# The MLP of a streaming encoder step as seven half-size block products instead of eight, tokens in halves, activations kept in DRAM

## The chip, the cores and the metric

The kernel runs on one core of one Trainium2 chip. The metric is the device time of one execution in microseconds (us). Its engines are TensorE (PE in the profile, its weight loads are PEld), VectorE (DVE), ScalarE (ACT), GpSimd (POOL) and SyncE (SP, which here only issues DMAs). Each engine takes its instructions in the order in which the program lists them.

## The reference

One layer of a hybrid encoder on 1024 prompt tokens and 32 sample tokens, in float32. What the change touches is the end of the layer:

```python
x = x + m                                    # m: output of the mixer
hm = rmsnorm(x, norm2_g[l]) @ w_mlp1[l]      # 1024 -> 4096
x = x + jnp.square(jax.nn.relu(hm)) @ w_mlp2[l]   # 4096 -> 1024
...
return rmsnorm(x, final_g), ...
```

## The kernel before

All activations are kept transposed: features on the 128 partitions, the 1056 tokens along the free axis. `R` holds the residual, 8 feature tiles by 1056 tokens. The tokens are taken in three chunks of 352 (`CW`).

The dense work is one stream of jobs. A job is a tile of 128 output features; its weights come as one DMA of 512 KB (`raw`), and are split into a high part `whi` (ACT, line 105) and the rest `wlo` (line 106, POOL at first, DVE in the second half of the program). The operand is split the same way, so that one float32 product becomes three passes (high by high, high by rest, rest by high). `group` (line 141) runs one job on one chunk: 8 tiles of the contraction by 3 passes, 24 matmuls of 352 columns into one of three PSUM banks; then the job's `evac` takes the sums out. `run` issues the loads and splits of the next two jobs ahead of a job's groups, and steps generators that stand beside the stream (`norm2`, `final`).

At the end of the program come 8 jobs for `w_o` (line 804: plus the input, into `R`; lines 213 and 214: split operands `h2`, by the gain of the norm; lines 789 to 793: sums of squares), then the MLP: four times 8 jobs of the first product (line 829: relu and the token's 1/rms; 831: square; 836 and 837: split into `u`) and 8 of the second (line 848: the sum is added into `R`). So the MLP is 64 jobs by 3 groups by 24 matmuls = 4608, and the last two jobs take their third chunk in halves of 176 columns. The hidden activations `u` stay on the chip, 1024 features at a time. Nothing of the residual goes through DRAM.

A token's 1/rms (`rstd_bc`) is a chain over four engines: small matmuls `st` (line 195), DVE `nv` (198), POOL `pow` into `nr` (200), DVE `dg` or `fbc` (204), matmuls `bc` (208).

The whole program stands in an order written out by hand; no scheduler moves anything.

Of the kernel before, what the change touches and what calls it, by code (L numbers as in the profile page):

```python
# [14 lines left out]
P = 128  # L15
# [5 lines left out]
NCH = 3  # L21
CW = T // NCH
HW = CW // 2
# [20 lines left out]
# Jobs beside the heads: conv pairs "c" and merge gates "g"; the first list stands before the heads, each other  # L44
# beside one head's retention.
# [13 lines left out]
def encoder_step(ctx: ExitStack, tc: tile.TileContext, xT, par_d, idn_d, cst_d, rot_d, w_in, w_co, w_ro,  # L59
                 w_o, w_1, w_2, sconv_d, sret_d, yT, oconv, oret):  # L60
    nc = tc.nc
    # Chunks of tokens; the last two are the halves of the third.
    cs = [slice(c * CW, (c + 1) * CW) for c in range(NCH)] + [slice(T - CW, T - HW), slice(T - HW, T)]
# [17 lines left out]
    ysp = [dram.tile([P, T], F32, name=f"ysp{i}") for i in range(8)]  # L81

# [25 lines left out]
    # Work beside the stream: generators that go on by a step after each group; those in `mids` also halfway.  # L108
# [9 lines left out]
    # Products whose evacuation waits for the first norm; ends of evacuations that come a group later.  # L118
    held, deferred, normed = [], [], [0]
    room = {}  # L120

# [4 lines left out]
    def group(n, c):  # L126
        j = jobs[n]
        xh, xl = j.rhs()
        if c < NCH:
            xh, xl, w = xh[c], xl[c], CW  # L130
        else:
            w = HW
            xh, xl = (a[NCH - 1][:, :, (c - NCH) * HW:(c - NCH + 1) * HW] for a in (xh, xl))
        ps = room.pop((n, c), None)
        if ps is None:
            ps = pm.tile([P, CW], F32, tag="pm", name=f"ps{n}_{c}")[:, :w]
# [15 lines left out]
    # Orders of two jobs' groups: chunk by chunk, and with the first job's end (and its weights' room) drawn forward.  # L152
# [3 lines left out]
    def run(count, order=None):  # L156
        """The next `count` jobs, job by job, or in the given order of (job, chunk)."""
# [53 lines left out]
    def gain_split(hi, lo, src, gcol):  # L211
        """src by the per-feature gain, split into hi and lo; the token's 1/rms comes after the product."""
# [26 lines left out]
    def finish(g):  # L239
        """What a generator returns at its end."""  # L240
# [6 lines left out]
    with tc.manual_schedule():  # L247
        xv = xT.rearrange("k p t -> p k t")
        with ExitStack() as ph:
# [43 lines left out]
            def gate_head(h):  # L293
                """The retention's own gate: swish, times the normed retention, in place."""
# [98 lines left out]
            def mm3(out, ws, xs, start, stop):  # L393
                """One product of split operands, as three passes."""
# [128 lines left out]
            def enter(c):  # L523
                """Chunk c's operands, and its squares."""
# [27 lines left out]
            def turn(c):  # L552
                """The rotary tables take the token's 1/rms."""
# [34 lines left out]
            # The jobs' order: conv pairs and merge gates around the heads' projections.  # L588
# [223 lines left out]
        def norm2():  # L812
            for _ in range(3):
                yield
# [201 lines left out]
```

## Time and profile before

| what | value |
| --- | --- |
| runs | 2277.15, 2277.15, 2273.67 us; median 2277.15 us |
| profiled execution | span 2274.5 us; no time of its own is listed beside the span |
| mean granted TensorE clock | 0.997 |
| steps of the `w_o` jobs | about 1430 to 1526 us |
| first split of `u` (line 836) | 1526.8 us |
| last matmul of the second product | 2262.6 us |

The profile's page gives busy time by engine, the span in 40 slices, the chain of work that ended last, and groups of instructions by line with the mean duration of one. A matmul's duration is longer than the distance to the next one, since they overlap; the rate is the number of them in a window. "Idle before" is how long an engine waited ahead of such an instruction, and for whom.

### The profile page before, as it was taken

What the parts mean: (1) busy time and instruction counts of PE and PEld (TensorE: products, weight loads), DVE (VectorE), ACT (ScalarE), POOL (GpSimd) and SP (SyncE); (2) the same over time, 40 slices, a digit from 0 to 9 for tenths busy, and PEclk for the clock granted to TensorE, in tenths of its full rate; (3) what the DMA queues carried; (4) which work ended last, traced back from release to release, by engine and by line L of the source; (5) the groups of instructions that cost most, each with busy time, mean ns of one, the idle gap of its engine ahead of it and who ended that gap; (6) DMA issues with size and microseconds to landing.
All of it is one profiled execution on the core that took longest, in us unless ns stands there. A gap on an engine that the chain in (4) does not pass through costs nothing.

```text
span 2274.5 us, 32748 instructions
## 1 busy us (share of the span) xinstructions
PE 2234.4 (98%) x13894; PEld 2190.3 (96%) x13894; DVE 1197.1 (53%) x1636; ACT 565.5 (25%) x969; POOL 759.0 (33%) x546
## 2 busy tenths in 40 slices
PE   7999999999999999999999999999999999999998
PEld 6999999999999999999999999999999999999998
DVE  7948885287943879359654663442222222222234
ACT  4113210132111321123243332333203202302321
POOL 4625465264642656436410542002102101201201
PEclk9999999999999999999999999999999999999999
DMA  4112122111211122211441333321111111111112
GB/s 165 50 45 67 39 103 75 38 57 59 100 59 48 48 68 84 66 48 56 162 167 57 128 111 95 95 66 47 47 47 47 47 47 47 47 47 47 47 47 77
DMA packets 60707, 159.12 MB, mean 70 GB/s; under 512 B 9744, under 2 KB 26384, under 8 KB 60560
## 3 DMA queue, kind: packets, MB, share of 16 engines
q1 hardware_dynamic: 60560, 157.02, 21.3%
q8 instruction: 109, 1.79, 0.3%
q14 instruction: 38, 0.31, 0.0%
HBM read 126.61 MB, written 30.39 MB: 69 GB/s over the span
## 4 chain that ended last, share of the span: by engine, by line
PE 87%; DVE 8%; issue 2%; POOL 1%; DMA 1%; ACT 0%; SPq 0%; DVEq 0%; ACTq 0%; POOLq 0%
PE ps L141 79%; DVE yc L364 4%; PE po L396 3%; PE pkv L396 2%; DVE o L305 1%; PE pto L490 1%; DVE h_lo L214 1%; POOL wlo L106 1%; PE pt L412 1%; PE pk L420 1%; DMA raw<-w_in 0%; DVE gsig L300 0%; DVE sq L539 0%; SPq L633 0%; PE pk L418 0%
## 5 line engine op out<-in xcount | busy, mean ns | idle before, releaser
L141 PE MATMUL ps<-h_hi,whi 128*128 128x352 f32 x1904 | 621.5, 326 | 7.9 <-ACT h_hi L213 6.7
L141 PE MATMUL ps<-h_hi,wlo 128*128 128x352 f32 x1904 | 615.9, 323 | 5.5 <-POOL wlo L106 4.8
L141 PE MATMUL ps<-h_lo,whi 128*128 128x352 f32 x1904 | 613.7, 322 | 0.7 <-DVE h_lo L214 0.7
L364 DVE SCALAR_TENSOR_TENSOR yc<-glu,par,yc 128x1086 f32<-128x1086 f32 x240 | 420.9, 1754 | 3.4
L141 PEld LDWEIGHTS ps<-h_hi,whi 128*128 128x128 f32 x1904 | 359.0, 189 | 12.1 <-ACT h_hi L213 6.7
L141 PE MATMUL ps<-u,whi 128*128 128x352 f32 (+1 forms) x1568 | 369.7, 320 | 0.0
L141 PEld LDWEIGHTS ps<-h_hi,wlo 128*128 128x128 f32 x1904 | 359.3, 189 | 7.8 <-POOL wlo L106 6.8
L141 PE MATMUL ps<-h,whi 128*128 128x352 f32 x1536 | 366.4, 322 | 0.0
L141 PEld LDWEIGHTS ps<-h_lo,whi 128*128 128x128 f32 x1904 | 360.7, 189 | 3.3 <-DVE h_lo L214 2.0
L105 ACT CAST whi<-raw 128x1024 fp32r<-128x1024 f32 x176 | 184.0, 1045 | 586.3 <-PE ps L141 469.1
L106 POOL TENSOR_TENSOR wlo<-raw,whi 128x1024 fp32r<-128x1024 f32 x80 | 232.4, 2906 | 193.7 <-ACT whi L105 193.7
L837 POOL TENSOR_TENSOR u<-uu,u 128x352 fp32r<-128x352 f32 x96 | 90.9, 947 | 551.8 <-ACT u L836 543.2
L141 PEld LDWEIGHTS ps<-u,whi 128*128 128x128 f32 x1568 | 269.4, 188 | 0.0
L141 PEld LDWEIGHTS ps<-h,whi 128*128 128x128 f32 x1536 | 265.2, 188 | 0.0
L141 PE MATMUL ps<-u,wlo 128*128 128x352 f32 (+1 forms) x784 | 249.4, 318 | 0.0
L141 PE MATMUL ps<-h,wlo 128*128 128x352 f32 x768 | 245.8, 320 | 0.0
L106 DVE TENSOR_TENSOR wlo<-raw,whi 128x1024 fp32r<-128x1024 f32 x96 | 117.9, 1228 | 127.7 <-ACT whi L105 118.8
L848 DVE TENSOR_TENSOR R<-ps,R 128x352 f32<-128x352 f32 (+1 forms) x98 | 50.6, 517 | 226.2 <-PE ps L141 226.2
L829 DVE SCALAR_TENSOR_TENSOR ur<-ps,rms 128x352 f32<-128x352 f32 x96 | 50.3, 524 | 214.1 <-PE ps L141 214.0
L141 PEld LDWEIGHTS ps<-u,wlo 128*128 128x128 f32 x784 | 147.0, 188 | 0.0
L141 PEld LDWEIGHTS ps<-h,wlo 128*128 128x128 f32 x768 | 143.9, 187 | 0.0
L831 ACT ACTIVATE uu<-ur 128x352 f32<-128x352 f32 x96 | 47.8, 498 | 245.8 <-DVE ur L829 245.8
(176 smaller groups left out, 3017.5 us busy)
## 6 DMA issues: line engine op xcount, KB each, us to landing
raw<-w_in SPq DMA_DIRECT2D x80, 512.0 KB, 4.1
raw<-w SPq DMA_DIRECT2D x64, 512.0 KB, 3.5
gate<-gt SPq DMA_DIRECT2D x16, 528.0 KB, 3.0
gsp<-o SPq DMA_DIRECT2D x16, 528.0 KB, 3.0
raw<-w_ro SPq DMA_DIRECT2D x16, 512.0 KB, 4.0
xt<-xT SPq DMA_DIRECT2D x12, 352.0 KB, 7.8
g0raw<-gsp SPq DMA_DIRECT2D x6, 704.0 KB, 9.8
gld<-gsp SPq DMA_DIRECT2D x12, 352.0 KB, 4.7
```

The source lines that it names most:

```text
L105: nc.scalar.copy(j.hi, j.raw)
L106: j.eng.tensor_tensor(out=j.lo, in0=j.raw, in1=j.hi.bitcast(F32), op=ALU.subtract)
L141: nc.tensor.matmul(ps, lhsT=a[:, k, :], rhs=x[:, k, :], start=(k == 0 and m == 0), stop=(k == KT - 1 and m == 2))
L214: nc.vector.scalar_tensor_tensor(out=lo, in0=src, scalar=pcol(gcol), in1=hi.bitcast(F32), op0=ALU.mult, op1=ALU.subtract)
L305: nc.vector.scalar_tensor_tensor(out=o[:, e, cs[c]], in0=y, scalar=pcol(O_GN + 4 * h + e), in1=t, op0=ALU.mult, op1=ALU.mult)
L364: nc.vector.scalar_tensor_tensor(out=y, in0=glu[:, t:t + YL], scalar=w, in1=y, op0=ALU.mult, op1=ALU.add)
L396: nc.tensor.matmul(out, lhsT=w, rhs=x, start=start and i == 0, stop=stop and i == 2)
L412: nc.tensor.transpose(pt[:n, e * P:(e + 1) * P], v[:, e, ts_], ident)
L829: nc.vector.scalar_tensor_tensor(out=r, in0=ps, scalar=0.0, in1=rms2[c], op0=ALU.max, op1=ALU.mult)
L831: nc.scalar.activation(out=u, in_=r, func=AF.Square)
L837: nc.gpsimd.tensor_tensor(out=lo[c][:, f, :], in0=u, in1=hi[c][:, f, :].bitcast(F32), op=ALU.subtract)
L848: nc.vector.tensor_tensor(out=R[:, f, cs[c]], in0=ps, in1=R[:, f, cs[c]], op=ALU.add)
```

## The change

The first product X1 = W1 X and the second Y = W2 U are each cut into blocks. A block product of the first one takes half of the contraction (4 tiles), half of the output features and half of the tokens (528); 2 by 2 by 2 halves would be eight block products, and Strassen's scheme in Winograd's form forms seven, from sums of blocks of the weights (S1 to S4) and of the operand (T1 to T4). A half of the tokens is run as two pieces of 264 columns (`s` = 0, 1), so one group is now 4 tiles by 3 passes = 12 matmuls of 264 columns.

- **`w_o`**: 16 jobs in place of 8, each on one half of the tokens (2 groups of 24 matmuls of 264 columns). `R` is also written to DRAM (`rsp`).
- **First product**: 16 pairs of feature tiles; a pair is 7 products by 2 pieces by 12 = 168 matmuls. The names are m*n*_*p**s*: pair n, product p, piece s. `operands` builds B22, T1 to T4 of the second token half from `R` (four differences of 128x4x264 on DVE, five splits on ACT with POOL or DVE) while products 1 and 2 of the first two pairs run; product 2 adds onto product 1 in the same PSUM bank, after ACT has copied product 1 out. From then on `R` is the place where the sums of a pair are collected (`U`, 8 tiles by 264): ACT takes relu and square, POOL forms the T sums, and one DMA writes them to DRAM (`usp`). The next pair uses the same place.
- **Second product**: 4 groups of features by 7 products = 28 slots, each 8 groups of 12 matmuls. The activations come back from DRAM (`xs`), are split on ACT, POOL and DVE; weight blocks are summed on DVE (`wsum`); the sums go into `R` and `acc` on DVE and POOL (`acc_r`, `acc_a`).
- The norm's gain is applied to `R` before the product, not after. The end (`ending`) is by quarters of 264 tokens.
- PSUM: five banks in turn in place of three.

```diff
-        h2 = [[], []]
...
+        def product(ps, w, x, fresh=True):
+
+            for k in range(QW):
+                for m, (a, b) in enumerate(((w[0], x[0]), (w[0], x[1]), (w[1], x[0]))):
+                    nc.tensor.matmul(ps, lhsT=a[:, k, :], rhs=b[:, k, :], start=(fresh and k == 0 and m == 0),
+                                     stop=(k == QW - 1 and m == 2), skip_group_check=not fresh)
+
+        def split2(w, src, eng):
+            nc.scalar.copy(w[0], src)
+            eng.tensor_tensor(out=w[1], in0=src, in1=w[0].bitcast(F32), op=ALU.subtract)
...
+        run_order = []
+        for n in range(2):
+            run_order += [(n, p, s) for p in (1, 2) for s in range(2)]
+        for n in range(2):
+            run_order += [(n, p, s) for s in range(2) for p in (3, 6, 5, 7, 4)]
+        for n in range(2, NPAIR):
+            run_order += [(n, p, s) for s in range(2) for p in (1, 6, 2, 5, 7, 3, 4)]
...
+                    def relu2():
+                        if n < 2:
+                            nc.scalar.activation(out=u[0], in_=e[:, 0], func=AF.Relu)
+                        nc.scalar.activation(out=U[:, 1:4], in_=U[:, 1:4], func=AF.Relu)
+                        nc.scalar.activation(out=U[:, 0:4], in_=U[:, 0:4], func=AF.Square)
+
+                    def ts():
+                        gt = nc.gpsimd.tensor_tensor
+                        gt(out=U[:, 4:6], in0=U[:, 1:3], in1=U[:, 0:2], op=ALU.subtract)
+                        gt(out=u[6], in0=u[2], in1=u[4], op=ALU.subtract)
+                        gt(out=u[7], in0=u[6], in1=u[3], op=ALU.subtract)
+                        nc.sync.dma_start(out=usp[n // 4][:, :, n % 4, s * ST:(s + 1) * ST], in_=U)
+                    hook(1, relu2)
+                    hook(2, ts)
...
+                scale_rows(range(4, 8), q, bc)
+                cut("B22", b22, nc.gpsimd)
+                if q == 2:
+                    next(rr[3])
+                scale_rows(range(4), q, bc)
+                tt(out=b11, in0=b12, in1=b11, op=ALU.subtract)
+                cut("T1", b11, nc.gpsimd)
+                tt(out=b12, in0=b22, in1=b12, op=ALU.subtract)
+                tt(out=b22, in0=b22, in1=b11, op=ALU.subtract)
+                tt(out=b21, in0=b22, in1=b21, op=ALU.subtract)
+                cut("T2", b22, nc.vector)
+                cut("T3", b12, nc.gpsimd)
+                cut("T4", b21, nc.vector)
...
+                if n >= 2 and s == 0:
+                    if p == 1:
+                        load_raw(m + 1)
+                        if n == 4:
+                            for f in range(8):
+                                nc.sync.dma_start(out=R[:, f, hs[0]], in_=rsp[f][:, hs[0]])
+                        prep_a(m)
...
+                elif p == 4:
+                    acc_r(i + 4, s, ps, ALU.subtract)
+                    if s == 1:
+                        acc_a(i + 4, i, 0)
+                        acc_a(i + 4, i, 1)
+                elif p == 7:
+                    acc_r(i + 4, s, ps)
+                    acc_r(i + 4, s + 2, ps)
+                    if s == 1:
+                        acc_a(i, i, 1)
...
+                if gi in (1, 2, 3, 5):
+                    k = (1, 2, 3, 5).index(gi)
+                    cut_x(j + 1, k, nc.vector if k == 3 else None)
...
+            for j, (g, p) in enumerate(slots):
+                final = j == len(slots) - 1
```

Three places in the order of the instructions matter below. The first is ACT around the start of the MLP. Before, after the last `w_o` job (`h2` is the operand, `sq` a square, `bc_n2` the broadcast 1/rms, `uu` and `u0` the hidden activation):

```order
L213 ACTIVATE h2_02_12959<-R_10285,par_66 128x352 [waits DVE_49]
L792 ACTIVATE sq_13679<-R_10285 128x352 [waits Activation_49]
L821 COPY rms2_13682<-bc_n20_13683 128x352 [waits PE_49]
L105 CAST whi113_13702<-raw113_13571 128x1024 [waits DMAHW7_49]
L831 ACTIVATE uu_13733<-ur_13731 128x352 [waits DVE_49,Activation_49]
L836 CAST u00_13735<-uu_13733 128x352 [waits Activation_49]
```

Now, from the copy of the last product-2 sum of pair 0 to the copies of pair 1 (`m1_10` is pair 1, product 1, piece 0; `xB22` to `xT4` are operands of the second token half, here its second quarter):

```order
L980 COPY early_14011<-m0_11_14049 128x264 [waits PE_49]
L857 CAST xB22_hi_13397<-R_10300 128x4x264 [waits DVE_49]
L857 CAST xT1_hi_14014<-R_10300 128x4x264 [waits DVE_49]
L857 CAST xT2_hi_14012<-R_10300 128x4x264 [waits DVE_49]
L857 CAST xT3_hi_14016<-R_10300 128x4x264
L857 CAST xT4_hi_14018<-R_10300 128x4x264 [waits DVE_49]
L977 COPY early_14011<-m1_10_14158 128x264 [waits PE_49]
L977 COPY early_14011<-m1_11_14172 128x264 [waits PE_49]
L980 COPY early_14011<-m1_10_14158 128x264 [waits PE_49]
```

The copies of pair 1's first sums now stand behind five splits that wait for DVE; before, an evacuation stood behind one copy and one weight split.

The second place is ACT in a later pair of the first product. Before, between two weight splits, there were only activations of the group just ended:

```order
L105 CAST whi131_15400<-raw131_15299 128x1024 [waits DMAHW1_49,PE_49]
L831 ACTIVATE uu_15431<-ur_15429 128x352 [waits DVE_49,Pool_49]
L836 CAST u00_15229<-uu_15431 128x352 [waits Activation_49]
L831 ACTIVATE uu_15462<-ur_15460 128x352 [waits DVE_49,Pool_49]
L836 CAST u01_15262<-uu_15462 128x352 [waits Activation_49]
```

Now, in pair 5 (line 977 copies product 1, 1003 and 1004 are relu and square of the piece before, 982 relu of product 2, `a6` and `xB11` are splits of weights):

```order
L977 COPY R_10300<-m5_10_15252 128x264 [waits DMAHW4_49,PE_49,Pool_49]
L857 CAST a6_hi_15270<-yy_10302 128x1024 [waits DMAHW1_49]
L1003 ACTIVATE R_10300<-R_10300 128x3x264 [waits DVE_49]
L1004 ACTIVATE R_10300<-R_10300 128x4x264 [waits Activation_49]
L982 ACTIVATE R_10300<-m5_10_15252 128x264 [waits PE_49]
L977 COPY R_10300<-m5_11_15368 128x264 [waits DMAHW7_49,PE_49,Pool_49]
L1003 ACTIVATE R_10300<-R_10300 128x3x264 [waits DVE_49]
L1004 ACTIVATE R_10300<-R_10300 128x4x264 [waits Activation_49]
L857 CAST xB11_hi_13393<-yy_10302 128x512 [waits PE_49]
```

Each copy of product 1 now also waits for a DMA (DMAHW), the write of the pair before out of the same place, and relu and square of the other piece stand behind it.

The third place is POOL in the second product, first group, around the slot of product 4 (line 858 with `u4`, `u5` splits the next slots' activations, line 1184 is `acc_a`). Before, POOL had no instruction in a job of the second product, apart from the norm's `nr` at the end. Now:

```order
L1184 TENSOR_TENSOR R_10300<-R_10300,yy_10302 128x528 [waits DVE_49]
L1184 TENSOR_TENSOR R_10300<-R_10300,yy_10302 128x528 [waits DMAHW5_49,DMAHW0_49]
L858 TENSOR_TENSOR u4_lo_18256<-xs_18097,u4_hi_18255 128x528 [waits DMAHW4_49,PE_49,Activation_49]
L858 TENSOR_TENSOR u4_lo_18256<-xs_18097,u4_hi_18255 128x528 [waits Activation_49]
L1184 TENSOR_TENSOR R_10300<-R_10300,yy_10302 128x528 [waits DVE_49]
L1184 TENSOR_TENSOR R_10300<-R_10300,yy_10302 128x528 [waits DMAHW6_49]
L858 TENSOR_TENSOR u4_lo_18256<-xs_18097,u4_hi_18255 128x528 [waits Activation_49]
```

The splits that the next slot's matmuls need stand in one queue with the additions of this slot.

More of the change, by code (lines that the diff above doesn't have):

```diff
@@ L120, in encoder_step, with bank @@
     room = {}
+    rings = [(pm, "pm", 3)]
+    turnof = [0]
+    def bank(name):
+        i = turnof[0] % sum(r[2] for r in rings)
+        turnof[0] += 1
+        for pool, tag, n in rings:
+            if i < n:
+                return pool.tile([P, CW], F32, tag=tag, name=name)
+            i -= n
     def flush(n):
@@ L687, in ro_evac1 @@
             return evac, pre
-        g1 = act(cp, "g1")
+        g1 = whole("g1")[1]
         for f in range(8):
@@ L795, in o_job, with add_square @@
-        def o_job(f):
+        qs = [slice(i * ST, (i + 1) * ST) for i in range(4)]
+        hs = [slice(0, HT), slice(HT, T)]
+        def add_square(f, sl, first, tmp):
+            if first:
+                nc.scalar.activation(out=ss[:, sl], in_=R[:, f, sl], func=AF.Square)
+            else:
+                nc.scalar.activation(out=tmp, in_=R[:, f, sl], func=AF.Square)
+                nc.vector.tensor_tensor(out=ss[:, sl], in0=ss[:, sl], in1=tmp, op=ALU.add)
+        HALF1 = (4, 5, 6, 7, 0, 1, 2, 3)
@@ L808, in evac @@
-                gain_split(h2[0][c][:, f, :], h2[1][c][:, f, :], r, O_N2 + f)
-                square_sum(f, c)
-            return Job(w_o[f], lambda: late["m"], evac, pre)
-        def norm2():
-            for _ in range(3):
-                yield
-            for c in range(NCH):
-                r = rstd_bc(t1("dg"), pn, ("pn", "pn"), ss[c], RMS_EPS, f"n2{c}")
-                next(r)
+                r = R[:, f, qs[c]]
+                nc.vector.tensor_tensor(out=r, in0=ps, in1=hold["t"][:, qs[c - 2 * half]], op=ALU.add)
@@ new lines, in evac, with hook @@
+                nc.sync.dma_start(out=rsp[f][:, qs[c]], in_=r)
+                add_square(f, qs[c], f == (0, 4)[half], t1("sq")[:, :ST])
+            return Job(w_o[f], lambda: [[x[:, :, q] for q in qs] for x in late["m"][0]], evac, pre)
+        for f in range(8):
+            jobs.append(o_job(f, 0))
+        for f in HALF1:
+            jobs.append(o_job(f, 1))
+        NG = FF // D
+        QW = KT // 2
+        step, hooks = [0], {}
+        def hook(ahead, fn):
+            hooks.setdefault(step[0] + ahead, []).append(fn)
@@ new lines, in encoder_step, with unit, last_pair @@
+        NAME = {1: "A11", 2: "A12", 3: "A12", 4: "A22", 5: "S1", 6: "A11", 7: "A21"}
+        def unit(u):
+            if u < 2 * len(slots):
+                g, p = slots[u // 2]
+                units[u] = [wp.tile([P, KT, P], F32R, tag=part, name=f"v{u}_{part}") for part in ("hi", "lo")]
+                split2(units[u], wq[g, NAME[p], u % 2], nc.vector)
+        def last_pair(p, s):
+            if s == 0 and p == 1:
+                load_xs(0, yy[:, :XW].rearrange("p (k t) -> p k t", k=QW))
+                for hf in range(2):
+                    load_quad(wp, "raw", 2, 0, "A11", hf)
+            if s == 1:
+                if p == 2:
+                    unit(0)
+                if p in (2, 5, 7, 3):
+                    cut_x(0, (2, 5, 7, 3).index(p))
```

514 lines of the change are left out of this document (394 added, 120 removed).

## The prediction

> **What bounds the kernel now.** First the page's engine rows, the row of slices and the chain that ended last:
>
> ```profile
> span 2274.5 us, 32748 instructions
> PE 2234.4 (98%) x13894; PEld 2190.3 (96%) x13894; DVE 1197.1 (53%) x1636; ACT 565.5 (25%) x969; POOL 759.0 (33%) x546
> PE   7999999999999999999999999999999999999998
> PEclk9999999999999999999999999999999999999999
> PE 87%; DVE 8%; issue 2%; POOL 1%; DMA 1%; ACT 0%; SPq 0%; DVEq 0%; ACTq 0%; POOLq 0%
> ```
>
> PE is busy in every slice at the full granted clock, and it holds 87% of the chain. In the MLP nothing else ends late: time there is the number of matmuls times their spacing. So the spacing comes next, from a window inside the MLP and from stretches of narrower and wider matmuls (columns of the window: its length; PE, PEld, DVE, ACT, POOL busy with counts; granted clock, DMA share, GB/s):
>
> ```profile
> 1600.00:1800.00 200.00, 200.00 (x1261) 200.00 (x1259) 48.36 (x70) 45.39 (x76) 26.51 (x28) 1.00 0.15 45
> 2257.12 0.28 PE L141 MATMUL ps<-u,wlo 128*128 128x176 f32 x1
> 2259.46 0.27 PE L141 MATMUL ps<-u,wlo 128*128 128x176 f32 x1
> 1091.20 0.40 PE L396 MATMUL po<-shi,q2lo 128*128 128x512 f32 x1
> 1093.25 0.39 PE L396 MATMUL pkv<-vthi,ktlo 128*128 128x512 f32 x1
> ```
>
> A matmul of 352 columns takes 200.00/1261 = 158.6 ns. The two rows of 176 columns stand 21 matmuls and 2.34 us apart: 111.4 ns. Those of 512 stand 9 and 2.05 us apart: 227.8 ns. DVE, ACT and POOL have 75% and more of the window free, so the second question is where the new order makes PE wait for them.
>
> **The change, term 1: fewer, narrower matmuls.** No row has 264 columns. From 352 to 512 the slope is 0.4325 ns a column, which carried down gives 120.5 at 264. A straight line between 176 and 352 gives 135.0; the row at 176 is the floor, 111.4. 352 and 176 are equally near. I take 121, since the upper line carried down to 176 would give 82.5, below its row: something other than columns sets the narrow case, and it sets in only below 243 columns if the two limits simply meet. The MLP was 4560 × 158.6 + 96 × 111.4 = 733.9 us. It is now twice 2688 matmuls, 5376 × 121 = 650.5. That is −83.4. `w_o` goes from 576 × 158.6 = 91.4 to 768 × 121 = 92.9, +1.5; the added matmuls of more norms, +2. **PE alone: −80.** At 111.4 it would be −139, at 135 +6.
>
> The Trainium skill, page "TensorE: Matmul & The Clock Gate", Part 2, section "Back-to-back issue gap", has N/2.4 + 2.5 ns for one warm matmul of N columns, thus 112.5 at 264 and an estimate of 605 us for the 5376, but that gives 149 at 352 where the window shows 158.6, and its sustained figure for 512 (about 131 ns) is far from the 227.8 here.
>
> **Term 2: the start of the MLP.** Prices of the pieces (mean of one):
>
> ```profile
> L105 ACT CAST whi<-raw 128x1024 fp32r<-128x1024 f32 x176 | 184.0, 1045 | 586.3 <-PE ps L141 469.1
> L106 DVE TENSOR_TENSOR wlo<-raw,whi 128x1024 fp32r<-128x1024 f32 x96 | 117.9, 1228 | 127.7 <-ACT whi L105 118.8
> L400 POOL TENSOR_TENSOR slo<-s,shi 128x1024 fp32r<-128x1024 f32 x28 | 70.1, 2503 | 34.8 <-ACT shi L399 34.8
> L883 DVE SCALAR_TENSOR_TENSOR R<-R,par,bc_fn 128x352 f32<-128x352 f32 x13 | 6.6, 574 | 0.0
> L883 DVE SCALAR_TENSOR_TENSOR R<-R,par,bc_fn 128x176 f32<-128x176 f32 x10 | 3.3, 390 | 0.5 <-ACT fbc L875 0.5
> L875 ACT COPY fbc<-bc_fn 128x176 f32<-128x176 f32 x2 | 0.6, 296 | 4.1 <-PE bc_fn L208 4.1
> L875 ACT COPY fbc<-bc_fn 128x352 f32<-128x352 f32 x1 | 0.4, 433 | 0.0
> L200 POOL TENSOR_TENSOR nr_n<-nv_n,mhalf 128x3 f32<-128x3 f32 x6 | 5.1, 851 | 97.8 <-DVE nv_n L198 95.2 <-PE more L141 2.6
> 1519.12 0.66 DVE L204 TENSOR_SCALAR dg<-ident,nr_n 128x128 f32<-128x128 f32 x3 [0.97 <-POOL nr_n L200]
> 28.00:30.00 2.00, 2.00 (x8) 2.00 (x8) 1.93 (x4) 0.97 (x1) 0.00 (x0) 0.50 0.00 0
> 30.00:40.00 10.00, 9.17 (x55) 8.73 (x55) 8.08 (x11) 5.70 (x11) 6.50 (x7) 0.94 0.00 1
> ```
>
> By size: a split of 1056 is 1.07 on ACT, 1.25 on DVE, 2.5 on POOL; a scaled row of 264 is 0.48, a block difference 1.25, an ACT copy of 264 0.37. I walk the queues from the last `w_o` matmul. The third quarter's `nv` stands on DVE behind four operations (0.45) and three of 512 (0.7): 3.9 us. Its `pow` stands on POOL behind the weight split wlo121, and is out at 7.6; `dg` 0.66 and the broadcast 0.7 give 9.0; four rows 10.9. B22 (1.07 on ACT, 2.5 on POOL) holds POOL to 14.5, so the fourth quarter's `pow` is out at 15.4, and its `dg`, which stands on DVE ahead of the remaining rows, at 16.1. Four rows and three differences: 21.8. ACT's three splits T2, T3, T4: 25.0. DVE's rests of T4 and A22: 27.0. The fourth quarter then has eight rows and three differences, 34.7; three splits on ACT, 37.9; and only behind these, by the order shown, the copy of pair 1's first sum: 38.4. Product 2 of pair 1 adds into that bank and needs the copy. PE has till then six groups (12 × 0.121 = 1.45 each) and the norms' matmuls, 10.5 us together. **So PE stands 27.9 us.** Nothing hides it: every product on offer needs the operands that are being built. After an idle stretch at the program's start the window at 28 us has the clock at 0.50 and the next ten at 0.94, so 1.0 + 0.6 us lost; I take 2. The first two quarters' broadcasts add 1. **+31**; half of it, 15, if POOL's queue happens to run early, 36 if POOL's splits take the 2.9 us of a mixed mean.
>
> **Term 3: the loop of the first product's write-back.** Fourteen of the sixteen pairs take their sums in one place per piece of tokens. The order shown makes a ring: copy of product 1 → weight split, relu and square of the other piece on ACT → POOL's T sums → DMA write → copy of the other piece → the same again. Rows for it:
>
> ```profile
> L532 POOL TENSOR_TENSOR sq<-xt 128x704 f32<-128x704 f32 x6 | 9.5, 1590 | 10.0 <-DMA xt<-xT 7.6 <-DVE rms L541 2.4
> L881 POOL TENSOR_TENSOR R<-R,fbc 128x176 f32<-128x176 f32 x6 | 3.2, 553 | 0.7 <-ACT fbc L875 0.7
> L837 POOL TENSOR_TENSOR u<-uu,u 128x352 fp32r<-128x352 f32 x96 | 90.9, 947 | 551.8 <-ACT u L836 543.2
> L534 ACT ACTIVATE sq<-xt 128x704 f32<-128x704 f32 x6 | 4.4, 780 | 0.0
> yT<-R SPq DMA_DIRECT2D x4, 264.0 KB, 2.7
> gsp<-o SPq DMA_DIRECT2D x16, 528.0 KB, 3.0
> yT<-R SPq DMA_DIRECT2D x2, 704.0 KB, 3.5
> 1601.31 0.48 ACT L836 CAST u<-uu 128x352 fp32r<-128x352 f32 x1
> 1601.87 0.94 POOL L837 TENSOR_TENSOR u<-uu,u 128x352 fp32r<-128x352 f32 x1 [2.87 <-ACT u L836]
> ```
>
> Per pair: two copies 0.74; the weight split 1.05; two relus of 792 columns 1.71; two squares of 1056, 2.14; the S2 split 0.62 on ACT and 1.24 on POOL; twice POOL's 528 and two 264 (1.27 + 0.75 + 0.75), 5.54; seven crossings at 0.08 (1601.31 + 0.48 to 1601.87), 0.56; and two writes of 1056 KB. A write of 264, 528 and 704 KB lands in 2.7, 3.0 and 3.5 us; carried on at the last slope, 4.5. I take 4.5 each; bounds 3.3 (hardly above 528 KB) and 6 (pieces spread over more of the queue). Ring: 13.6 + 9.0 = 22.6 us. PE needs 168 × 0.121 = 20.3. With 12.5 pairs bound by it, 2.3 × 12.5 = **+29**. A microsecond of landing is worth 2 a pair, 25 in all, and below 3.3 the ring stops deciding. Reloading half of `R` ahead of pair 4 lets the ring wait one landing more, **+3.5**.
>
> **Term 4: the second product.** A slot is 96 × 0.121 = 11.6 us on PE, four groups of seven slots.
>
> ```profile
> L757 POOL TENSOR_TENSOR z<-yt,z x24: 942/1194/1949, 1248.1 to 1344.9; 128x352 fp32r<-128x352 f32 x24
> 1250.00:1300.00 50.00, 50.00 (x318) 49.79 (x317) 36.73 (x61) 18.05 (x35) 25.59 (x25) 1.00 0.40 130
> L848 DVE TENSOR_TENSOR R<-ps,R 128x352 f32<-128x352 f32 x94 | 49.3, 524 | 224.9 <-PE ps L141 224.9
> L848 DVE TENSOR_TENSOR R<-ps,R 128x176 f32<-128x176 f32 x4 | 1.4, 340 | 1.3 <-PE ps L141 1.3
> ```
>
> In the two slots of products 4 and 7 POOL has 8 and 4 `acc_a` and three splits each, 18 operations of 528 columns, and the splits feed the next slot. At 1.27 they are 22.9 us against 23.2: no stall. But POOL's 352 columns, 942 ns at best, have a mean of 1194 where DVE is 73% busy, and a worst of 1949. At the full ratio 1.61 us: 5.8 late a group; I take 1.45, halfway, as DVE is less busy here: 26.1, or 2.9 a group, **+12** in four (0 to 44). Weights of the first slot +2, the change of phase +1.
>
> At the end DVE has in the slot before the last 16 sums (0.43), 8 additions of squares (0.4), two weight splits (1.23), a split and two scaled rows of 528 (0.7) and the norm's chains (3): about 17 us for 11.6 of PE; **+6** (0 to 12), as part is worked off in the last slot.
>
> **Sum**: −80 + 31 + 29 + 3.5 + 12 + 3 + 6 = +4.5. The profiled execution's span is 2274.5, 2.65 under the median of the runs, 2277.15; the difference is put on the median: 2281.7, with roundings upwards (a hop here and there) 2283.
>
> **The rivals.**
> - *The write lands early and the ring doesn't bind* (3.3 us or less): for it, doubling 264 to 528 KB cost only 0.3; against, 176 KB more cost 0.5. It takes the +29 away: **2254**, faster.
> - *Matmuls at the floor of 111.4.* Inside the ring-bound part nothing is gained; on 2688 + 768 outside, 9.6 ns each is −33: **2250**. Against it, 352 and 512 both stand well above their column time at 176.
> - *POOL overloads the second product*: at 1.9 us, the worst `z`, 18 operations are 34.2, 11 late a group, 44 in place of 12: **2315**. It decides from 1.29 us an operation. For it the spread of `z`; against, its mean.
> - The Trainium skill, page "SBUF — State Buffer", section "SBUF: two separate sides", says that a DVE operation with two SBUF inputs and a GpSimd operation that reads SBUF lock each other out for the whole instruction; with an estimated 8.8 us of such DVE work in the two slots that would be 8.5 late a group, +34 in place of 12, and the `z` row's spread speaks for it, as it does for the rival above.
> - *The write lands in 6 us*: 25.6 a pair, +66 in place of 29: **2320**. For it, 1056 KB is larger than any write seen.
> - *The narrower matmuls save nothing* (135.0 ns): +86, less the ring's 29, since a pair is then 22.7: **2340**.
>
> **How the numbers follow.** Forecast 0.40 (own range 2262 to 2305: the start's 15 and 36, the landing a half microsecond either way, POOL from 1.35 to 1.6); ring free 0.21; floor 0.05; POOL 0.16; slow write 0.14; 135 ns 0.04. A measurement of this kernel can tell about 0.2%, 4.6 us, from no change. The forecast's own 0.40 parts into 0.08 faster, 0.15 within, 0.17 slower; the first two rivals are faster; the last three slower, 0.01 of them within by offsetting gains. Faster 0.34, same 0.16, slower 0.50. The range 2240 to 2325 takes in all but the 135 ns case and the tails of the others.
>
> **What would show it.** Inside a piece's products the spacing of 264 columns should be near 121 ns. At the start of the MLP PE should stand once for over 20 us, ending with the copy of pair 1's first sum, then a half clock. Between pairs the period should be 22.6 with PE waiting for line 977, and that for the write of `usp` with a landing of 4.5. In the slots of products 4 and 7 lines 858 and 1184 on POOL should take 1.45 and the next slot wait for line 858. A pair period of 20.3, a stall at the start under 15, or POOL's operations at 1.27 or 1.9 would each make it wrong by the price given.

## The result, and the profile after

The changed kernel takes 2357.74 us (median of 4 runs, 2355.79 to 2359.36) where the kernel before took 2275.77 in the same comparison: a ratio of 1.0359, with a 95% interval of 1.0345 to 1.0374. It is 3.6% slower. The forecast was 2283, and the range ended at 2325.

The page of the changed kernel, the lines that answer to those of before (engine rows, slices, chain, two groups of part 5 and two rows of part 6):

```profile
span 2357.6 us, 35930 instructions
PE 2208.8 (94%) x14826; PEld 2153.0 (91%) x14826; DVE 1511.0 (64%) x2130; ACT 695.0 (29%) x1155; POOL 1091.0 (46%) x739
PE   7999999999999999999999999948988888999996
PEclk9999999999999999999999999969999999999998
PE 65%; DVE 12%; POOL 9%; issue 7%; DMA 5%; ACT 2%; SPq 0%; POOLq 0%; ACTq 0%; DVEq 0%
L858 POOL TENSOR_TENSOR u_lo<-xs,u_hi 128x528 fp32r<-128x528 f32 x81 | 130.9, 1636 | 105.2 <-ACT u_hi L857 101.2
L1180 DVE TENSOR_TENSOR R<-d,R 128x264 f32<-128x264 f32 x224 | 88.5, 424 | 56.8 <-PE d L853 32.8
usp<-R SPq DMA_DIRECT2D x32, 1056.0 KB, 5.3
xs<-usp SPq DMA_DIRECT2D x27, 1056.0 KB, 4.9
```

PE's share of the chain falls from 87% to 65%, and POOL, DVE and DMA take what it lost. From slice 27 on (1530 us) PE is no longer busy throughout: one slice with a 4 where the MLP starts, and mostly 8s for the rest of the first product. Where the stretches begin and end is read from the first and last start of a few groups of PE's rows (a view by tile: duration in ns, least, median and longest; first and last start), and from one row of the timeline:

```profile
L853 PE MATMUL m<-xB_hi,whi x32: 282/376/589, 1529.3 to 1579.6; 128*128 128x264 f32 x32
L853 PE MATMUL m<-xB_hi,a_hi x224: 280/285/588, 1615.4 to 1960.6; 128*128 128x264 f32 x112
L853 PE MATMUL d<-u_hi,v_hi x896: 278/285/567, 1966.8 to 2344.1; 128*128 128x264 f32 x180
2285.01 0.28 PE L853 MATMUL d<-u_hi,v_hi 128*128 128x264 f32 x1
```

The MLP starts at 1529.3, pair 2 at 1615.4, the second product at 1966.8; the matmul at 2285.0 is the first of the last three slots (288 matmuls are left). Each stretch less its matmuls at the 0.121 us of the prediction:

| stretch | us | matmuls | over PE's work | forecast |
| --- | --- | --- | --- | --- |
| start, pairs 0 and 1 | 86.1 | 336 | 45 | 31 |
| pairs 2 to 15 | 351.4 | 2352 | 67 | 32.5 |
| second product, first 25 slots | 318.2 | 2400 | 28 | 15 |
| last three slots and tail, less the tail of before (11.9) | 60.7 | 288 | 26 | 6 |
| sum | | | 166 | 84.5 |

Every stretch went over in the direction forecast: by nearly half as much again at the start, by about twice in the two long stretches, and by four times at the end. The saving in PE's own work came as forecast. In the `w_o` jobs, and in a run in which nothing else binds the first product (e1, below), windows show:

```profile
1475.00:1500.00 25.00, 25.00 (x209) 24.85 (x207) 14.77 (x31) 7.07 (x11) 4.18 (x3) 1.00 0.50 166
1700.00:1800.00 100.00, 100.00 (x812) 99.21 (x811) 50.16 (x94) 43.27 (x66) 50.96 (x44) 1.00 0.48 162
```

That is 119.6 and 123.2 ns for a matmul of 264 columns.

### The profile page after: what moved, and what is told of

Same layout as the page of the kernel before. It is cut to its first block, busy times and chain, and to the rows that moved or that the text cites. A ratio compares the mean times of both kernels' runs of the same rounds, so it can differ in the third digit from the quotient of the medians.

```text
span 2357.6 us, 35930 instructions
## 1 busy us (share of the span) xinstructions
PE 2208.8 (94%) x14826; PEld 2153.0 (91%) x14826; DVE 1511.0 (64%) x2130; ACT 695.0 (29%) x1155; POOL 1091.0 (46%) x739
## 4 chain that ended last, share of the span: by engine, by line
PE 65%; DVE 12%; POOL 9%; issue 7%; DMA 5%; ACT 2%; SPq 0%; POOLq 0%; ACTq 0%; DVEq 0%
PE ps L151 45%; PE m L853 8%; PE d L853 4%; DVE yc L374 3%; DMA usp<-R 3%; PE po L406 3%; POOL R L1184 2%; POOL u_lo L858 2%; PE pkv L406 2%; POOL xB_lo L858 1%; POOL R L1008 1%; DVE o L315 1%; PE pto L500 1%; DVE h_lo L224 1%; POOL R L1010 1%
## 5 line engine op out<-in xcount | busy, mean ns | idle before, releaser
L853 PE MATMUL d<-u_lo,v_hi 128*128 128x264 f32 x896 | 260.4, 291 | 18.9 <-POOL u_lo L858 18.9
L853 PE MATMUL d<-u_hi,v_lo 128*128 128x264 f32 x896 | 260.5, 291 | 3.6 <-DVE v_lo L858 3.4
L853 PE MATMUL d<-u_hi,v_hi 128*128 128x264 f32 x896 | 260.4, 291 | 2.2 <-ACT v_hi L857 2.2
L853 PEld LDWEIGHTS d<-u_lo,v_hi 128*128 128x128 f32 x896 | 173.6, 194 | 21.5 <-POOL u_lo L858 21.4
L858 POOL TENSOR_TENSOR u_lo<-xs,u_hi 128x528 fp32r<-128x528 f32 x81 | 130.9, 1636 | 105.2 <-ACT u_hi L857 101.2
L853 PEld LDWEIGHTS d<-u_hi,v_lo 128*128 128x128 f32 x896 | 173.8, 194 | 5.5 <-DVE v_lo L858 5.5
L853 PEld LDWEIGHTS d<-u_hi,v_hi 128*128 128x128 f32 x896 | 173.6, 194 | 2.4 <-ACT v_hi L857 2.4
L853 PE MATMUL m<-xT_hi,xB_lo 128*128 128x264 f32 x384 | 114.0, 297 | 4.6 <-POOL xB_lo L858 4.6
L853 PE MATMUL m<-xT_hi,xB_hi 128*128 128x264 f32 x384 | 114.6, 298 | 0.0
L853 PE MATMUL m<-xT_lo,xB_hi 128*128 128x264 f32 x384 | 113.9, 297 | 0.0
```

The source lines that it names most:

```text
L853: nc.tensor.matmul(ps, lhsT=a[:, k, :], rhs=b[:, k, :], start=(fresh and k == 0 and m == 0), stop=(k == QW - 1 and m == 2), skip_group_che ...
L858: eng.tensor_tensor(out=w[1], in0=src, in1=w[0].bitcast(F32), op=ALU.subtract)
```

## The experiments

All runs are edits of the changed kernel. "Against changed" is the median less 2357.74. The runs of one kernel lie 3 to 10 us apart, and the intervals of e2, e3, e5 and e12 overlap that of the changed kernel (1.0345 to 1.0374): those four show no gain.

| run | edit | us | against before, 95% interval | against changed |
| --- | --- | --- | --- | --- |
| e1 | relu, square, T sums and write at once | 2301.14 | 1.0102 to 1.0132 | -56.6 |
| e11 | the write in two halves | 2304.67 | 1.0117 to 1.0146 | -53.1 |
| e5 | product 6 computed twice | 2354.35 | 1.0331 to 1.0365 | -3.4 |
| e2 | fourth quarter's operands later | 2355.66 | 1.0326 to 1.0363 | -2.1 |
| e3 | low halves of three operands on DVE | 2355.61 | 1.0337 to 1.0367 | -2.1 |
| e4 | POOL's additions held back | 2347.24 | 1.0298 to 1.0329 | -10.5 |
| e12 | PE's wait in product 4's slot filled | 2357.35 | 1.0350 to 1.0378 | -0.4 |
| e6 | e1 + e2 + e4 | 2291.14 | 1.0049 to 1.0081 | -66.6 |
| e7 | e6, other order at the end | 2294.59 | 1.0059 to 1.0095 | -63.2 |
| e8 | e6, held-back additions on DVE | 2284.63 | 1.0026 to 1.0050 | -73.1 |
| e9 | e8 with three waits taken away | 2274.49 | 0.9988 to 1.0005 | -83.3 |
| e10 | e9 with e3's splits, T1 later | 2269.59 | 0.9969 to 0.9990 | -88.2 |

### The ring of the first product: e1, e11, e5

The timeline of the changed kernel over one pair (start, duration, engine, line, operation; in brackets the idle time before and who ended it), ACT first, then POOL and SyncE:

```profile
1720.20 0.87 ACT L1003 ACTIVATE R<-R 128x792 f32<-128x792 f32 x1
1721.10 1.08 ACT L1004 ACTIVATE R<-R 128x1056 f32<-128x1056 f32 x1
1730.98 0.38 ACT L977 COPY R<-m 128x264 f32<-128x264 f32 x1 [8.42 <-DMA usp<-R]
1744.00 0.38 ACT L977 COPY R<-m 128x264 f32<-128x264 f32 x1 [4.48 <-DMA usp<-R]
...
1722.26 1.42 POOL L1008 TENSOR_TENSOR R<-R 128x528 f32<-128x528 f32 x1 [5.71 <-ACT R L1004]
1723.75 1.08 POOL L1009 TENSOR_TENSOR R<-R 128x264 f32<-128x264 f32 x1
1724.92 1.09 POOL L1010 TENSOR_TENSOR R<-R 128x264 f32<-128x264 f32 x1
1737.31 1.09 POOL L1010 TENSOR_TENSOR R<-R 128x264 f32<-128x264 f32 x1
...
1726.03 12.92 SPq L1011 DMA_DIRECT2D usp<-R  x2
```

Read it as a ring: relu and square end at 1722.2, POOL's three sums take 3.75 us, the write is issued at 1726.03, and the copy that waits for it starts at 1730.98. Behind this copy stand relu and square of the other piece, whose sums end at 1738.40 and whose write lets the next copy go at 1744.00. Two landings, 4.95 and 5.60 us, stand in one pair. e1 opens the ring by order alone, e11 by the size of the write that is waited for, and e5 asks whether PE is the bound at all. The period of the pair shown is 25.0 us (an earlier copy went at 1718.98), and 25 of the 28 copies of product 1 in pairs 2 to 15 waited for the write.

e1:

```diff
-                    hook(1, relu2)
-                    hook(2, ts)
+                    hook(0, relu2)
+                    hook(0, ts)
```

> Changed kernel, with relu and square (lines 1003, 1004) and the T sums with their write (1008 to 1011) put right behind the last product of a piece, ahead of the next piece's copy of product 1, in place of one and two groups later. Ring theory (the pairs of the first product are bound by copy, relu, square, T sums, write, each piece's behind the other's): the two pieces no longer wait for each other, a pair falls from 25.0 us to 20.1 to 21, the 40 us that PE waits for line 977 are nearly gone; time 55 to 70 us below the changed kernel (about 2290 to 2305). Rival (the write of 1056 KB itself is the limit, it only starts earlier and lands as late because the queue is full): less than 20 us gained, and line 977 still waits for usp.

e11:

```diff
-                        nc.sync.dma_start(out=usp[n // 4][:, :, n % 4, s * ST:(s + 1) * ST], in_=U)
+                        for a in (4, 0):
+                            nc.sync.dma_start(out=usp[n // 4][:, a:a + 4, n % 4, s * ST:(s + 1) * ST], in_=U[:, a:a + 4])
```

> Changed kernel, with the write of a piece's sums as two DMAs of 528 KB, the half that holds product 1's place first. Ring theory with the landing as its largest term: the copy of product 1 waits for the first half alone, 3.0 to 3.7 us in place of 5.3, a pair is 3 to 4.6 us shorter, 35 to 60 us below the changed kernel. Rival (what counts of the landing is a fixed part, the same for a smaller write): within 15 us of the changed kernel.

e5:

```diff
+                if n >= 2 and p == 6:
+                    product(ps, W, [a[:, :, qs[s]] for a in xop[x]], True)
                 product(ps, W, [a[:, :, qs[s]] for a in xop[x]], p != 2)
```

> Changed kernel, with product 6 of pairs 2 to 15 computed twice into the same bank (the first pass is overwritten): 28 x 12 = 336 more matmuls, 40 us more work for PE at the 119.6 ns seen. Ring theory: PE is not the bound of these pairs, the pair stays at 25.0 us, time within 8 us of the changed kernel. Clock theory (PE loses its time because the granted clock falls to half after each wait, the waits alone are small): with the waits filled the clock stays full, 10 to 25 us less time. If PE is the bound: 40 us more.

From pair 2's first product to pair 15's last product 2 there are 13.7 pairs. The same group of PE's rows that marks pair 2 above, in e1, e11 and e5, in that order:

```profile
L853 PE MATMUL m<-xB_hi,a_hi x224: 280/285/391, 1607.9 to 1896.3; 128*128 128x264 f32 x112
...
L853 PE MATMUL m<-xB_hi,a_hi x224: 280/285/393, 1611.8 to 1905.4; 128*128 128x264 f32 x112
...
L853 PE MATMUL m<-xB_hi,a_hi x224: 279/286/393, 1610.7 to 1953.3; 128*128 128x264 f32 x112
```

A pair takes 345.2/13.7 = 25.2 us in the changed kernel, 21.1 in e1, 21.4 in e11, and 25.0 in e5. So e5's 336 more matmuls, some 40 us of PE's work, cost nothing. The windows say it directly, the changed kernel first, e5 second:

```profile
1600.00:1950.00 350.00, 307.04 (x2315) 301.57 (x2316) 157.63 (x267) 125.00 (x195) 154.27 (x128) 0.94 0.41 141
...
1600.00:1950.00 350.00, 335.84 (x2690) 330.19 (x2690) 156.33 (x269) 124.99 (x196) 154.26 (x126) 1.00 0.41 141
```

PE runs 375 more matmuls in the same 350 us, at a clock of 1.00 in place of 0.94, while DVE, ACT and POOL do the same amount. The bound was the ring, neither PE nor its clock. e1 removes it by letting each piece's work go ahead of the other's copy; e11 leaves the order and shortens the landing that is waited for, and gains nearly as much. With e1's order PE's waits for line 977 sum to 0.9 us, from 40.3. e11's rival fell too: the landing of a smaller write is shorter. The copy goes 3.1 us after the first half's issue (1708.93 to 1712.07 in e11), though the median of both halves of 528 KB, which share the queues, is 4.1 us (3.0 for writes of that size earlier in the program).

### The start: e2, e3

e2 builds the fourth quarter's operands later:

```diff
-                elif i == 3:
+                elif i == 7:
                     operands(3, finish(rr[3]))
...
-            for i in (1, 3):
+            for i in (1, 7):
```

> Changed kernel, with the operands of the fourth quarter built four groups later (behind the last product 2 of pair 1 in place of behind that of pair 0). Queue theory of the start (the copy of pair 1's first sum stands behind the fourth quarter's five splits): that copy comes right behind the third quarter's splits, PE starts again at about 1560 in place of 1575 and runs seven groups (10 us) with the operands it has, before it waits for the fourth quarter; 6 to 12 us below the changed kernel, the time divided into two waits. Rival (the start is bound by DVE's work on both quarters, whatever stands in ACT's queue): the second wait gives back all, within 4 us.

The 6 to 12 us did not come. PE's long wait, first as it was, then the waits of e2:

```profile
1574.83 0.59 PE L853 MATMUL m<-xB_hi,whi 128*128 128x264 f32 x1 [25.60 <-ACT early L977]
...
1558.95 0.59 PE L853 MATMUL m<-xB_hi,whi 128*128 128x264 f32 x1 [9.54 <-ACT early L977]
1579.39 0.59 PE L853 MATMUL m<-xB_hi,wS_hi 128*128 128x264 f32 x1 [7.13 <-ACT R L994]
1597.59 0.46 PE L853 MATMUL m<-xT_hi,xB_lo 128*128 128x264 f32 x1 [4.05 <-POOL xB_lo L858]
```

The copy came early as expected (9.5 us of wait in place of 25.6), but 7.1 came back at once, since the sums of pair 0 stand behind the fourth quarter's splits, and 4.1 later. The start got shorter all the same: 80.3 us (1530.4 to 1610.7) in place of 86.1. But pairs 2 to 15 took 353.9 us in place of 351.4, and the 2.1 us left over for the kernel are inside the noise. The forecast's path (third and fourth quarter one behind the other, then the copy) was the right one; moving the copy off it mostly divides the wait. Why pairs 2 to 15 took part of the gain back is not shown.

e3 moves three splits:

```diff
-                cut("B22", b22, nc.gpsimd)
+                cut("B22", b22, nc.vector)
...
-                cut("T1", b11, nc.gpsimd)
+                cut("T1", b11, nc.vector)
...
-                cut("T3", b12, nc.gpsimd)
+                cut("T3", b12, nc.vector)
```

> Changed kernel, with the low halves of B22, T1 and T3 of the second token half (three of five per quarter) formed on DVE in place of POOL. Theory of the shared port (a DVE operation with two operands in SBUF stands while a POOL operation runs): line 1037 falls from 3.31 us to 1.3, line 1034 of the fourth quarter from 3.08 to 1.3, and though DVE gets 7.5 us more work PE's stall at the start is 2 to 6 us shorter. Rival (DVE stood there for data): these durations stay above 3 us and the stall is 4 us or more longer.

The timeline of the changed kernel (a difference on DVE, and what POOL does meanwhile), then the same difference in e3:

```profile
1549.59 3.31 DVE L1037 TENSOR_TENSOR R<-R 128x1056 f32<-128x1056 f32 x1
...
1549.38 2.40 POOL L858 TENSOR_TENSOR xT_lo<-R,xT_hi 128x1056 fp32r<-128x1056 f32 x1 [4.73 <-ACT xT_hi L857]
...
1549.66 1.26 DVE L1037 TENSOR_TENSOR R<-R 128x1056 f32<-128x1056 f32 x1
```

In the changed kernel DVE's operation starts 0.2 us after POOL's, and ends 1.1 us after POOL's end: it stood for POOL's whole instruction and then did its own work. With POOL empty it takes 1.26 us. The Trainium skill, page "SBUF — State Buffer", section "SBUF: two separate sides", says this of DVE operations with two operands in SBUF beside a GpSimd operation that reads SBUF; the trace agrees (3.31 us against 1.26). The time hardly moved (PE's wait 25.4 for 25.6), which fits DVE now doing the work that it had waited for (7.5 us by the expectation). So the mechanism is shown, this edit alone gains nothing that can be measured, and the "2 to 6 us" was wrong. In e10, where T1's split also stands behind the differences rather than between them, the move is worth 4.9 us against e9, nearly all of it at the start (74.2 us, 1526.3 to 1600.5, where e9 took 78.6). Which of the two edits did it was not separated.

### The second product: e4, e12, e8

e4 holds POOL's additions back, in the first three groups:

```diff
-                        acc_a(i + 4, i, 0)
-                        acc_a(i + 4, i, 1)
+                        later(lambda: acc_a(i + 4, i, 0))
+                        later(lambda: acc_a(i + 4, i, 1))
...
-                        acc_a(i, i, 1)
+                        later(lambda: acc_a(i, i, 1))
...
+                    if p in (5, 3) and gi >= 2 and held_a:
+                        held_a.pop(0)()
```

> Changed kernel, with the additions of line 1184 on POOL held back in the first three groups of the second product: the 12 of products 4 and 7 are issued one by one in the slots of products 5 and 3, where POOL has three splits only. Queue theory (the splits for the next slot stand behind the additions): the wait of 3.4 us for line 858 at the start of product 7's slot is gone in the first three groups, and with it some 2 us of half clock each; 10 to 16 us below the changed kernel. Rival (POOL is slow in itself in this phase, since DVE holds it up): the waits turn up in later slots, within 5 us of the changed kernel.

e12 fills the wait in place of removing it:

```diff
                     evac(p, i, s, ps)
+                    if p == 4 and gi == 7:
+                        px = bank(f"x{j}")[:, :ST]
+                        for _ in range(2):
+                            product(px, [a[:, 4 * (i % 2):4 * (i % 2) + 4] for a in w], [a[:, :, qs[s]] for a in xo[j]])
```

> Changed kernel, with the last group of product 4's slot computed twice more into a bank that nobody reads, in each of the four groups: 24 matmuls, 2.9 us, which lie in the 3.4 us that PE stands there for POOL's split. Clock theory (a wait of that length costs more than itself, since the granted clock is half for the next 18 matmuls or so, 0.22 us apart in place of 0.12): the clock stays full behind it, 1.5 to 2 us less per group, 5 to 8 us below the changed kernel although PE has 11.5 us more to do. Rival (the spacing there is set by late operands, not by the clock): 0 to 4 us above the changed kernel.

One wait of the changed kernel and the clock behind it (windows of 2 us), then the same wait in e12; last the wait that is left in e4:

```profile
2111.82 0.39 PE L853 MATMUL d<-u_lo,v_hi 128*128 128x264 f32 x1 [3.39 <-POOL u_lo L858]
2200.62 0.39 PE L853 MATMUL d<-u_lo,v_hi 128*128 128x264 f32 x1 [3.39 <-POOL u_lo L858]
...
2198.00:2200.00 2.00, 0.00 (x0) 0.00 (x0) 0.83 (x3) 0.96 (x2) 2.00 (x2) 1.00 0.00 0
2202.00:2204.00 2.00, 2.00 (x11) 2.00 (x11) 2.00 (x3) 0.00 (x0) 2.00 (x2) 0.50 0.83 313
...
2110.00 0.39 PE L853 MATMUL d<-u_lo,v_hi 128*128 128x264 f32 x1 [0.49 <-POOL u_lo L858]
2198.84 0.39 PE L853 MATMUL d<-u_lo,v_hi 128*128 128x264 f32 x1 [0.49 <-POOL u_lo L858]
...
2157.28 0.59 PE L853 MATMUL d<-u_hi,v_lo 128*128 128x264 f32 x1 [2.93 <-DVE v_lo L858]
2243.98 0.39 PE L853 MATMUL d<-u_hi,v_lo 128*128 128x264 f32 x1 [2.93 <-DVE v_lo L858]
```

After the wait the clock is at 0.50, 11 matmuls in 2 us where 19 are usual. In e12 the wait is filled, and in the window of this group the clock rises from 0.98 to 1.00. Yet the group takes 2198.84 - 2110.00 = 88.84 us, as before (88.80). The clock theory fell: what PE gains at full clock it waits away at the next hand-over (2.07 us at 2123.97). The group is bound by POOL and DVE. e4 takes 2.1 us out of it (86.70), and 10.5 in all, the low end of what the queue theory expected; then the wait is DVE's, so both theories are half right.

e8 puts the held-back additions on DVE:

```diff
-                nc.gpsimd.tensor_tensor(out=r, in0=r, in1=acc[:, i, :], op=ALU.add)
+                (nc.gpsimd if last_g[0] else nc.vector).tensor_tensor(out=r, in0=r, in1=acc[:, i, :], op=ALU.add)
```

> e6 with the held-back additions of line 1184 on DVE in place of POOL (12 x 0.7 = 8.5 us more on DVE for each of three groups, 12 x 1.5 less on POOL). Theory of the shared port: DVE's work that stood while POOL ran goes down by as much as is added, PE's waits for v_lo (2.9 us a group in e4) shrink; 4 to 10 us below e6. Rival (DVE is simply full): the waits for v_lo grow, 5 to 15 us above e6.

One group of e6, then one of e8 (columns as in the prediction: the window's length; PE, PEld, DVE, ACT and POOL busy with counts; clock, DMA share, GB/s):

```profile
2014.28:2099.45 85.17, 82.11 (x672) 81.69 (x672) 68.00 (x102) 32.17 (x50) 54.85 (x33) 1.00 0.39 139
...
2072.22:2156.76 84.54, 82.38 (x673) 81.76 (x673) 72.45 (x114) 32.37 (x50) 34.71 (x21) 1.00 0.40 140
```

The 12 additions take DVE 11.0 us here (0.92 each), but its busy time grows by 4.5 only: the 102 operations that it had before take 61.4 us in place of 68.0, with POOL less busy beside them. PE's waits for `v_lo` fall from 2.93 to 1.48 us, the first 25 slots take 310.7 us in place of 316.4, and the kernel is 6.5 us under e6. So the shared port is borne out, though DVE's other work went down by 6.5 us and not by as much as was added.

### Together, and the end: e6, e7, e9, e10

> The edits of e1 (relu first), e2 (fourth quarter late) and e4 (additions on POOL late) together. If the three prices are independent their gains add: 57 + 6 to 12 + 10 us below the changed kernel, 2278 to 2285 us, about the kernel before. If the clock or the shared port ties them together, it is 2288 or more.

The gains of e1, e2 and e4 add up to 69.2, together they give 66.6. At 2291 the kernel lies on the side that the expectation gave to prices tied together (2288 or more), but only because it had counted 6 to 12 us for e2, whose run gave 2.1. Against the measured sum the 2.6 us that are missing are less than the runs of one kernel differ, so a tie between the prices is not shown.

e7 begins the norm of the first half two groups later, and issues the last weight split early:

```diff
-                    if gi == 1:
+                    if gi == 3:
                         begin(0)
-                    elif gi == 2:
+                    elif gi == 4:
                         begin(1)
...
+                if gi == 7 and j == len(slots) - 2:
+                    unit(2 * j + 3)
```

> e6 with the norm of the first two quarters at the end begun two groups later, its output rows moved accordingly, and the last weight split issued ahead of the squares of the slot before. Theory of the end (DVE is behind in the last two slots, so that PE waits 2.8 us for the sums of squares and 2.9 us for a weight split, each followed by 3 to 7 us of half clock): both waits shrink, 6 to 10 us below e6. Rival (the work itself on DVE sets the end): within 3 us of e6.

Nothing was gained: 3.5 us over e6, less than the runs of this kernel differ (2289.27 to 2298.61). The wait for the weight split was gone, but the norm of the third quarter then waited 5.1 us for its sums. That fits the rival, DVE's work itself as the bound of the last slots. e9 keeps the early split alone, and takes two other waits away:

```diff
+                (nc.gpsimd if last_g[0] and (f < 4 or half == 0) else nc.vector).tensor_tensor(out=r, in0=r, in1=acc[:, i, :], op=ALU.add)
...
-                    hook(0, ts)
+                    hook(1 if (n, s) == (NPAIR - 1, 1) else 0, ts)
```

> e8 with three waits taken away that its trace shows: the second halves of product 4's additions of the last group on DVE (PE waits 3.4 us for POOL there), the last weight split issued in the slot before (2.7 + 0.7 us), and the last piece's T sums and write one group later, so that the load of the second slot's activations no longer stands behind that write in SyncE's queue (5.0 us). With 2 to 3 us of half clock behind each: 12 to 17 us below e8, 2268 to 2273 us, 0.2 to 0.4% faster than the kernel before. Rival (other work is late right behind each of them): 3 to 6 us below e8, still slower than before.

10 us under e8, a little less than expected, and level with the kernel before. By the traces most of it lies ahead of the end: the first 25 slots take 300.0 us in place of 310.7, the last three with the tail 71.3 in place of 75.1, where the changed kernel has 72.6.

> e9 with B22, T1 and T3 of the second token half split on DVE, T1 behind the four differences. Theory of the shared port: line 1037 at 1.26 us again, DVE's way through both quarters shorter by 3 to 6 us, as much below e9. Rival (ACT's splits, not DVE, are the chain of the start): within 2 us of e9.

e10 is 0.21% faster than the kernel before (0.10 to 0.31%), the only version that is. The same groups of PE's rows as in the result, and its first matmul of the last three slots, at 2195.25 of a span of 2267.4:

```profile
L853 PE MATMUL m<-xB_hi,whi x32: 282/287/586, 1526.3 to 1556.6; 128*128 128x264 f32 x32
L853 PE MATMUL m<-xB_hi,a_hi x224: 280/286/392, 1600.5 to 1888.6; 128*128 128x264 f32 x112
L853 PE MATMUL d<-u_hi,v_hi x896: 278/285/567, 1894.8 to 2254.5; 128*128 128x264 f32 x180
```

| stretch | changed, us | e10, us | over PE's work: changed | e10 | forecast |
| --- | --- | --- | --- | --- | --- |
| start, pairs 0 and 1 | 86.1 | 74.2 | 45 | 34 | 31 |
| pairs 2 to 15 | 351.4 | 294.3 | 67 | 10 | 32.5 |
| second product, first 25 slots | 318.2 | 300.4 | 28 | 10 | 15 |
| last three slots and tail, less 11.9 | 60.7 | 60.2 | 26 | 25 | 6 |

The first three stretches gave back 12, 57 and 18 us. The end gave back nothing.

## Why the prediction was wrong

The path of each stretch was the right one, and its price too low: the ring by 34.5 us, the end by 20, the start by 14, the second product by 13.

- **What bounds, and term 1 (matmuls)**: right. 119.6 to 123.2 ns were seen for 121; the rivals of 111.4 and 135.0 ns are out.
- **Term 3 (the ring)**: the mechanism was right, link by link, and it is the term that was furthest off: 32.5 forecast, 67 measured. The step that failed is its prices. "Carried on at the last slope, 4.5" for a landing was 4.95 and 5.60 in the pair shown and 5.3 in the median. POOL's sums, 5.54 for two pieces, were 7.1: three of the four operations of 264 columns took 1.08 to 1.09 us and one 0.76, where 0.75 had been taken. The landings are 1.55 us a pair longer, POOL's sums 1.5, the other links 0.7 shorter: 25.0 in place of 22.6. And "12.5 pairs bound by it" were nearly all fourteen. e5, e11 and e1 settle that this ring, and nothing of PE, was the price. The 3.5 for reloading half of `R` is too high: the copies before, at and behind pair 4 (1643.36, 1668.36, 1694.11, 1718.98) stand 25.0, 25.7 and 24.9 us apart, so it cost about 0.8.
- **Term 2 (the start)**: the copy named did end the wait, and 25.6 us is close to the 27.9 forecast. That is luck, since both ends of the wait were late:

```profile
1528.57 0.28 PE L151 MATMUL ps<-m_mh,wlo 128*128 128x264 f32 x1
1574.40 0.65 ACT L977 COPY early<-m 128x264 f32<-128x264 f32 x2
1555.98 2.78 DVE L858 TENSOR_TENSOR xT_lo<-R,xT_hi 128x1056 fp32r<-128x1056 f32 x1 [0.62 <-ACT xT_hi L857]
1563.66 3.08 DVE L1034 TENSOR_TENSOR R<-R 128x1056 f32<-128x1056 f32 x1
1537.09 1.42 PE L218 MATMUL bc_n<-ss,ones 128*128 128x128 f32 x6 [4.63 <-DVE ss L214]
```

  The copy was done 46 us after the last `w_o` matmul (first row) in place of 38.4. Four DVE operations beside POOL (3.31 twice, 3.08, 2.78, at 1.25 us each in the prediction) are 7.5 us of the difference. PE got there with 20.6 us of work and waits in place of 10.5: it had waited 4.6 for the third quarter's `dg`, and then ran at half the clock. Behind pair 1's copy it waited another 3.3 for operands. Some 70 matmuls of the start stood 0.22 us apart, 8 us more than at full clock, where the sum had 2. Together 45 in place of 31.
- **Term 4 (second product)**: forecast 15, measured 28. "I take 1.45, halfway" for POOL's 528 columns; the splits had a mean of 1.64. The point at which POOL decides, 1.29, was passed by far: with 1.64 the prediction's own sum is 6.3 us late a group in place of 2.9, and the group took 88.8 us against 81.3 of PE's work, 7.5 late. The rival of the lock, at 8.5 a group, was nearer than the forecast. e4 and e8 show POOL's queue and DVE's standing beside it, each a part.
- **The end**: forecast 6, "as part is worked off in the last slot". It was 26. In the last three slots PE waited 3.7 us for POOL's splits, 3.5 for the sums of squares and 3.2 for weight splits, and 73 matmuls ran at half the clock, 7.5 us more than at full. DVE's backlog was named; that PE's waits there would bring the half clock was left out. e7 and e9 were aimed at the end, but the last three slots with the tail took 73.5 and 71.3 us there and 72.2 in e10, for 72.6. So no run gave this loss back, and how it parts into DVE's own work, its standing beside POOL and the clock stays open.
- **The half clock** was counted once, at the start. It showed up behind many waits, but e5 and e12 say that it cost nothing in the two long stretches, because PE had to wait there anyway. That it was left out was no error there; at the start it was counted too low, and what it is worth there and at the end was not tried.
- **The rivals** were priced one by one and given as alternatives: slow write +37, POOL +32. They do not exclude each other, and both came in part: a landing of 5.3 us where the rival had 6, POOL at 1.64 where it had 1.9. 2283 and both prices would have been 2352. The range was built as if only one could happen. A common cause is not shown: e3 and e8 show DVE standing beside POOL, but while a write ran from 1742 to 1744 neither was busy.

The runs account for the loss in three of the four stretches: e10's edits give back 57 us of 67 in pairs 2 to 15 (e1 alone takes that stretch from 351.4 to 294.7), 18 of 28 in the second product and 12 of 45 at the start. The 20 us by which the end missed the forecast are not accounted for.

## What to carry to other kernels

When PE's work falls by a tenth, every link beside it is measured against the shorter time: work out the ring of waits with the durations seen while the neighbours are busy, not the best ones, and let rivals that don't exclude each other come together in the range. A term that comes out near its forecast still needs both its ends compared, as the wait at the start shows. Where one place in memory is filled, read out by a DMA and filled again, two edits without any new buffer are worth trying first: issue what feeds the write ahead of the instruction that waits for the last one, and split the write so that the part waited for goes first. Extra dummy work on the engine that seems to bind (e5, e12) tells in one run whether it does.

## What the runs showed of the hardware

- A DVE operation on 1056 columns with both operands in SBUF took 3.31 us beside a POOL operation of 2.40 us and 1.26 us without it (e3).
- The granted clock was 0.50 for some 3 to 8 us after many of PE's waits, and the length of the wait alone did not decide it. In the changed kernel a wait of 3.39 us (at 2200.62) and one of 2.32 us (at 1719.41) were followed by 0.50, one of 2.50 us (at 1744.44) stayed at 1.00. In e4 the two waits of 2.93 us that are shown above, at the same place of two groups, were followed once by 0.50 (2157.28) and once by 1.00 (2243.98). Behind the waits of 2.32 and 2.50 us:

```profile
1720.00:1722.00 2.00, 2.00 (x11) 2.00 (x11) 1.67 (x3) 1.97 (x3) 0.00 (x0) 0.50 0.51 209
...
1742.00:1744.00 2.00, 0.00 (x0) 0.00 (x0) 0.00 (x0) 0.00 (x0) 0.00 (x0) 1.00 1.01 336
1746.00:1748.00 2.00, 2.00 (x19) 2.00 (x18) 1.97 (x4) 1.46 (x3) 0.71 (x1) 1.00 0.00 0
```

  The Trainium skill, page "TensorE: Matmul & The Clock Gate", Part 1, section "What's actually happening", has the clock at half after an idle window of about 3.4 us that runs freely. That equal waits ended differently fits a window that runs freely; that 2.32 us were enough does not fit a whole window of 3.4 us. No run here shows the window itself.
- While a write of 1056 KB ran, with loads of weights beside it, the queues moved 336 GB/s (second row above). As two writes of 528 KB the halves landed in a median of 4.1 us, against 5.3 for the whole, and the copy that waited for the first half went 3.1 us after its issue.
